# HGRN and mLSTM layer on one core: the second half of the gates' chain one head later, and the low halves of the split weights by VectorE alone

## The chip, the cores and the metric

The kernel runs on 1 core of one Trainium2 chip. The metric is device time in microseconds (us); for one core it is the time of that core. The engines in the text are TensorE (PE, with PEld for its weight loads), VectorE (DVE), ScalarE (ACT), GpSimd (POOL) and SyncE (SP, which issues the DMAs of the weights). All times are us unless marked ns.

## The reference

One layer over 256 latent and 256 context tokens of 1024 channels, all in float32:

```python
sh1, sc1, g1, sh2, sc2, g2 = modulation(c, w_ada, b_ada)       # silu(c) @ w_ada, 6 x 1024
h_lat = rms_norm(x, norm1_g) * (1 + sc1) + sh1                  # the context likewise
p_lat = split(h_lat @ w_in + b_in, SEG_OFFSETS)                 # 13 segments
o_ctx, hs = hgrn_core(p_ctx[0:4], 0)                            # 8 heads, two directions
o_lat     = hgrn_core(p_lat[0:4], hs)                           # S_t = diag(f_t) S_t-1 + k_t v_t
r_ctx, ms = mlstm_core(p_ctx[5:10], 0)                          # 4 heads, conv of width 5 on q and k,
r_lat     = mlstm_core(p_lat[5:10], ms)                         # gates li, lf: cumsum and running max
y = sigmoid(p[11]) * (y_a @ w_branch_a) + sigmoid(p[12]) * (y_b @ w_branch_b)
x = x + g1 * (y @ w_out)
x = x + g2 * hier_moe(rms_norm(x, norm2_g) * (1 + sc2) + sh2)   # 32 experts, top 2 of one group of 8
out = rms_norm(x, final_norm_g)
```

## The kernel before

The program has five stages, which are seen in the trace one behind the other: the prologue (0 to 62 us: norm, first modulation, first weights); the HGRN branch (62 to 300) as four pairs of heads, `hgrn(gp, p, fin)` for p = 0 to 3; the mLSTM branch (300 to 450) as four heads, `mlstm(gp, h, fin)` for h = 0 to 3; the two branch projections, the merge, the output projection and the routing (450 to 575); and the 32 experts (575 to the end), which stream their weights.

**Weights in two halves.** Up to the experts every weight block (128 partitions x 2048 float32, 1 MB, tile `raw`, loaded through SP's queue) is multiplied in three passes: `load_split_` makes a rounded high half `whi` by two ACT copies of 1024 columns (L155), and the low half `wlo = raw - whi` by a subtraction (L158). The subtraction is divided among two engines by `kp`: DVE takes the first 256 * (8 - kp) columns, POOL the rest. `KH`, `MKP` and `GKP` are the `kp` of the HGRN, the mLSTM and the merge blocks. PE then runs `whi` against the high and low halves of the activations (L362 and L363, or L371 and L372 where the tokens are the stationary side) and last `wlo` against the high half (L365, L374). `whi` and `wlo` have two buffers each.

**A pair of HGRN heads** reads five blocks: two for the forget gates (tiles `sg`, `fl`, `fc` on DVE, `kl`, `kc` on POOL), `q`, `v`, and the output gate `s4`. Then `kd` (a scan `scn` on DVE, a product, four transposes on PE at L698 into the PSUM tile "tp") gives the state of the context, and eight levels combine the tokens of the latent sequence: at each, DVE multiplies `xa` (L759) and `kl` (L762), and PE multiplies them (L720, L744, L755). `fin` closes the pair (squares, column sums at L354, `rsn` by DVE L341 and POOL L342, spread by PE L348, then the scaled output) and is issued inside the next pair.

**The modulation pieces.** The rest of w_ada is multiplied on DVE along the way: `ada_dve(b, gp)` loads two blocks and issues eight operations on `adac` (L315 and L317, 128 x 512), and `post`, issued later by `ada_flush`, transposes the sum on PE into "tp" and reduces it on DVE (L326, tile `mod`). "tp" is one PSUM buffer: what PE transposes next into it waits for that reduce. `ADP` says at which place of a pair a chunk stands.

**The gates' chain.** `ml_gates` computes the log gates of all four mLSTM heads as rows of a 40-partition tile (`gz`, in the code `xf`, `li`, `lf`, `fs`): part 1 the logs, part 2 scans, part 3 `r` (`r1`), `R`, `rr`, and `r2`, part 4 the remaining scans, the exponentials on ACT, and the DMA of `rr` to HBM. `ml_cols` transposes the results (through "tp") for the mLSTM heads.

**What sets the order.** A scheduler orders each engine's instructions by priority and by data; `prio(n)` raises or lowers a group, and `tc.issue_after(i)` keeps what stands under it behind instruction i. In the kernel before, parts 1 and 2 of the chain stand behind the gates of p = 2 (`anchor[0]`, `anchor[1]`), and parts 3 and 4 behind the low half of that pair's last block (`anchor[2]`), that is, ahead of its `kd` and its levels.

**An mLSTM head** reads three blocks: q and k (conv, `cz`, on DVE, sigmoid on ACT), v, and the output gate. PE transposes k (L897), ACT makes `wk`, PE multiplies by v, DVE copies the state (`cs`, L908), and PE reads it at L949; the scores (`ex`) follow at L952.

Of the kernel before, what the change touches and what calls it, by code (L numbers as in the profile page):

```python
# [7 lines left out]
F32 = mybir.dt.float32  # L8
# [6 lines left out]
ALU = mybir.AluOpType  # L15
# [4 lines left out]
NQ = NE // 4  # L20
CAP = 32
RZ, RP, RA, RB, RC = 2, 2, 2, 5, 7
KH, MKP, GKP = 2, 3, 2
NWARM, NW0 = 2, (7, 2, 1)
MLG = 2
ADP = (1, 3)
# [115 lines left out]
def view(a, off, pat):  # L142
    return bass.AP(tensor=a.tensor, offset=a.offset + off, ap=[a.ap[0]] + pat)


def body(ctx, tc, A, out, dbg=None):
# [10 lines left out]
    def tt(o, a, b, op, e=None):  # L157
        return (e or V).tensor_tensor(o, a, b, op=op)  # L158

    def prio(n):  # L160
        return tc.high_priority(PRIO[n]) if PRIO[n] else nullcontext()
# [57 lines left out]
    def load_split(src, kp=4, pr="ls_h"):  # L219
        with prio(pr):  # L220
            return load_split_(src, kp)
# [368 lines left out]
    def ml_cols(rs):  # L590
        tps = pmm("tp")
        for a, r_ in enumerate(rs):
            for i in range(2):
                T.transpose(tps[:, 128 * (2 * a + i):128 * (2 * a + i) + 128], r_[:, 128 * i:128 * i + 128], ident)
        act(mlr.rearrange("p a i n -> p (a i n)"), tps, AF.Copy)
# [4 lines left out]
    yah = wp.tile([128, 8, 256], F32R, name="yah", tag="yh")  # L600
    yal = wp.tile([128, 8, 256], F32R, name="yal", tag="yl")

    anchor = []

    def hgrn(gp, p, fin):
        wb = [A["win"][5 * p + j] for j in range(5)]
        bcol = lambda j, m: 10 * p + 2 * j + m
        def ada_at(i):
            for j in range(2):
                if p and ADP[j] == i and 2 + 2 * p + j < 9:  # L610
                    ada_dve(2 + 2 * p + j, gp)

        fl = h1.tile([128, 2, 512], F32, name="fl", bufs=HB)
# [28 lines left out]
                    G.tensor_scalar(kc[:, d, m, :], sn[:, 256:512], oml[:, d, h:h + 1], None, op0=ALU.mult)  # L642
        anchor[:] = [ga.ins, gv.ins]
        ada_at(0)
        w = load_split(wb[2], KH)
        r = pmm("mm")
        q = h1.tile([128, 512], F32, name="q", bufs=1)
# [13 lines left out]
        for i in range(2):  # L661
            r = pmm("mm")
            for j in range(2):
                mm_tok(r[:, 256 * j:256 * j + 256], w, 256 * i + 128 * j)
            tt(v[:, 2 * i:2 * i + 2, :], r.rearrange("p (j n) -> p j n", j=2), br[:, None, :].to_broadcast([128, 2, 256]),
               ALU.add)
        ada_at(1)
        w = load_split(wb[4], KH)
        anchor.append(lolast[0])
        r4 = pmm("mm")  # L670
        s4 = gp.tile([128, 512], F32, name="s4")
        for m in range(2):
# [53 lines left out]
        with prio("lev"):  # L726
            for lv in range(8):
# [28 lines left out]
                    act(acr.rearrange("p a b -> p (a b)"), r, AF.Copy)  # L756
                tb = tot[:, 0, :]
                xv = view(xa[:, 0, :], 0, [[2 * h, 256 // h], [h + 512, 2], [1, h]])
                V.tensor_tensor(xv, xv, view(tb, 1, [[2, 256 // h], [n - 1, 2], [0, h]]), op=ALU.mult)  # L759
                if lv < 7:  # L760
                    yv = view(kl[:, 0, :], 0, [[2 * h, 256 // h], [h + 512, 2], [1, h]])
                    V.tensor_tensor(yv, yv, view(tb, n + 1, [[2, 256 // h], [-n - 1, 2], [0, h]]), op=ALU.mult)  # L762
# [1 line left out]
                    tv = tot.rearrange("p a (n t) -> p a n t", t=2)  # L764
                    tt(t, tv[:, :, :, 0], tv[:, :, :, 1], ALU.mult)
                    tot, n = t, n // 2
        ada_at(3)
        po = pmm("oo")
        for m in range(2):
            o = po[:, 256 * m:256 * m + 256]  # L770
# [28 lines left out]
    with ExitStack() as st:  # L799
        gp = pool(st, "hg")  # L800
        for n, w, b in ([("adac", 512, 1), ("scn", 514, 1), ("kd", 512, 1), ("kt", 512, 1)]
                        + [(f"tot{i}", 512 >> i, 1) for i in range(7)]
                        + [("yk", 512, 2), ("v", 1024, HB), ("s0", 512, 1), ("acr", 512, 1), ("ain", 512, 1), ("adg", 128, 1), ("xa", 1024, 1),
                           ("s4", 512, 1), ("t2", 512, 4)]):
            gp.tile([128, w], F32, name=n, bufs=b)
        zt = gp.tile([128, 256], F32, name="zt")
        G.memset(zt, 0.0)
        lm = gp.tile([128, 5, 32], U8, name="lm")
        lmf = gp.tile([128, 160], F32, name="lmf", tag="v", bufs=HB)
        D.dma_start(lmf, A["lmask"])  # L810
        V.tensor_copy(lm.rearrange("p a b -> p (a b)"), lmf)
        fin = None
        for p in range(4):
            fin = hgrn(gp, p, fin)
            if p == MLG:
                mlrows = []
                gates = ml_gates(mlrows)
                with prio("mlg"), tc.issue_after(anchor[0]), tc.issue_after(anchor[1]):
                    next(gates)
                    next(gates)  # L820
                with prio("mlg"), tc.issue_after(anchor[2]):
                    for _ in gates:
                        pass
                ml_cols(mlrows)
        fin()
        ada_flush()
    h1st.close()
# [14 lines left out]
    def mlstm(gp, h, fin):  # L842
# [13 lines left out]
        q = gp.tile([128, 256], F32, name="q", bufs=2)  # L856
        k = gp.tile([128, 2, 256], F32, name="k", bufs=2)
        with prio("conv"):
            for src, dst, ct in ((qin[:, None, :], q[:, None, :], h), (kin, k, 4 + h)):
                a = dst.shape[1]  # L860
                cw = lambda j: P["cw"][:, 5 * ct + j:5 * ct + j + 1]
                z = gp.tile([128, 2, 256], F32, name="cz")
                z = z[:, 0:a, :]
                V.tensor_scalar(z, src[:, :, 0:256], cw(0), P["cb"][:, ct:ct + 1], op0=ALU.mult, op1=ALU.add)
                for j in range(1, 5):
                    V.scalar_tensor_tensor(z, src[:, :, j:j + 256], cw(j), z, op0=ALU.mult, op1=ALU.add)
                act(dst, z, AF.Sigmoid)
                conv = tt(dst, dst, z, ALU.mult)
        w = load_split(wb[1], MKP, "ls_m")
        br = gp.tile([128, 256], F32, name="br", bufs=2)  # L870
        D.dma_start(br, A["brow"][1024 + 256 * h:1024 + 256 * h + 256].partition_broadcast(128))
# [8 lines left out]
        if fin is not None:  # L880
            fin()
        ada_flush()
        if h % 2 == 0:
            g2acc[0] = gp.tile([128, 512], F32, name="adac")
        with tc.issue_after(conv.ins):
            ada_dve(9 + h // 2, gp, g2acc[0], (h % 2,))
        w = load_split(wb[2], MKP, "ls_m")
        r = pmm("mm")
        s10 = gp.tile([128, 2, 256], F32, name="s10")
# [14 lines left out]
        for d in range(2):  # L904
            rc = pmm("oo")
            for i in range(2):
                T.matmul(rc[:, 0:257], wk[:, d, i, :], v[:, i, :], start=(i == 0), stop=(i == 1))
            V.tensor_copy(cs[:, d, :], rc[:, 0:257])  # L908

        sp = pmm("lv")  # L910
        for i in range(2):
# [573 lines left out]
```

## Time and profile before

| | |
|---|---|
| median of 3 runs | 1005.48 us (1004.79 to 1009.0) |
| profiled execution | 1005.86 us, span 1003.8 us (2.06 us lie around the span) |
| mean granted PE clock | 0.922 |
| busy in the span | PE 862.8, PEld 591.7, DVE 477.0, ACT 277.9, POOL 191.2 us |
| `whi` on ACT | x104, 1052 ns of one |
| `wlo` on DVE, on POOL | x54, 2004 ns of one; x50, 2254 ns of one |

Durations are those of the one profiled execution. A bracket behind an instruction gives how long its engine stood idle before it, and what ended that. A busy PE isn't PE at its peak: where the granted clock is below 1.00, the same matmuls take longer.

### The profile page before, as it was taken

The page shows a single profiled execution, that of the slowest core. Times are in us where ns is not written, and L with a number is a line of the kernel's source. Part 1 is how long each engine was busy: PE and PEld are TensorE (multiplying, and loading weights), DVE is VectorE, ACT ScalarE, POOL GpSimd, SP SyncE. Part 2 cuts the span into 40 slices and gives each one's busy share as a digit, 9 for nine tenths or more (in the row PEclk, how much of TensorE's full clock was granted, in tenths as well). Part 3 has the DMA queues.
Part 4 walks back from the last instruction along what each step waited for, and adds up shares of the span by engine and source line. Part 5 has one row for each costly group of instructions (what it writes and reads, how often), then busy time and mean ns, then how long its engine had stood idle before and what let it go on. Part 6 is the DMA issues. An engine that isn't in the chain of part 4 may idle for free.

```text
span 1003.8 us, 15963 instructions
## 1 busy us (share of the span) xinstructions
PE 862.8 (86%) x6687; PEld 591.7 (59%) x6687; DVE 477.0 (48%) x908; ACT 277.9 (28%) x430; POOL 191.2 (19%) x130
## 2 busy tenths in 40 slices
PE   7999999979998999999999999767686767777865
PEld 3588897968978898999999644213031220313312
DVE  3678779798667988874465422102020110202002
ACT  4564433643323553444443210000000000000101
POOL 0053441535503232124434000000000000000000
PEclk9999999989999999999999999879778776978978
DMA  9733345255243445248887999999999999999996
GB/s 372 287 130 133 126 137 193 98 191 187 96 164 114 165 147 167 83 159 321 300 332 277 373 423 426 426 425 423 428 424 427 425 424 388 419 426 424 426 424 265
DMA packets 45610, 290.50 MB, mean 289 GB/s; under 512 B 5216, under 2 KB 10336, under 8 KB 11104
## 3 DMA queue, kind: packets, MB, share of 16 engines
q1 hardware_dynamic: 45248, 288.94, 72.8%
q8 instruction: 53, 0.87, 0.3%
q10 hardware_dynamic: 288, 0.52, 0.1%
q14 instruction: 21, 0.17, 0.0%
HBM read 288.23 MB, written 1.21 MB: 288 GB/s over the span
## 4 chain that ended last, share of the span: by engine, by line
issue 45%; PE 41%; DVE 8%; ACT 3%; DMA 2%; POOL 1%; SPq 0%; POOLq 0%; DVEq 0%; ACTq 0%
PE mm L365 5%; PE mm L362 5%; PE mm L363 5%; PE mm L374 2%; PE mm L372 2%; PE mm L371 2%; PE mm L1102 2%; PE mm L1099 2%; PE mm L1100 2%; DMA raw<-in_win_dram 2%; PE mm L412 2%; DVE wlo L158 1%; PE mm L1240 1%; ACT whi L155 1%; PE oo L952 1%
## 5 line engine op out<-in xcount | busy, mean ns | idle before, releaser
L158 POOL TENSOR_TENSOR wlo<-raw,whi 128x512 fp32r<-128x512 f32 (+1 forms) x50 | 112.7, 2254 | 197.4 <-ACT whi L155 166.3
L155 ACT ACTIVATE whi<-raw 128x1024 fp32r<-128x1024 f32 x104 | 105.6, 1052 | 104.6 <-POOL wlo L158 26.3
L362 PE MATMUL mm<-hhi,whi 128*128 128x256 f32 (+1 forms) x448 | 132.2, 322 | 0.0
L363 PE MATMUL mm<-hlo,whi 128*128 128x256 f32 (+1 forms) x448 | 130.1, 317 | 0.0
L158 DVE TENSOR_TENSOR wlo<-raw,whi 128x1536 fp32r<-128x1536 f32 (+2 forms) x54 | 108.1, 2004 | 34.1 <-ACT whi L155 30.6
L158 DVE TENSOR_TENSOR a<-a,mm 128x512 f32<-128x512 f32 x8 | 5.5, 688 | 233.5 <-PE mm L1240 233.5
L362 PEld LDWEIGHTS mm<-hhi,whi 128*128 128x128 f32 x448 | 85.5, 191 | 4.8
L363 PEld LDWEIGHTS mm<-hlo,whi 128*128 128x128 f32 x448 | 85.5, 191 | 4.4
L1378 POOL TENSOR_TENSOR rsn<-rsn,con 128x2 f32<-128x2 f32 x1 | 0.7, 698 | 434.7 <-DVE rsn L158 434.7
L365 PE MATMUL mm<-hhi,wlo 128*128 128x256 f32 (+1 forms) x448 | 80.7, 319 | 0.9 <-POOL wlo L158 0.9
L365 PEld LDWEIGHTS mm<-hhi,wlo 128*128 128x128 f32 x448 | 65.8, 191 | 5.8 <-POOL wlo L158 1.1
L1214 DVE SCALAR_TENSOR_TENSOR x<-oo,mod,x 128x256 f32<-128x256 f32 x56 | 24.4, 480 | 88.3 <-PE oo L1273 88.3
L1240 PE MATMUL mm<-ub,xg 128*32 128x512 f32 x304 | 50.3, 734 | 17.3 <-DMA ub<-in_eu_dram 9.9
L371 PE MATMUL mm<-whi,hhi 128*128 128x256 f32 x256 | 63.1, 284 | 0.0
L372 PE MATMUL mm<-whi,hlo 128*128 128x256 f32 x256 | 62.9, 283 | 0.0
L371 PEld LDWEIGHTS mm<-whi,hhi 128*128 128x128 f32 x256 | 49.1, 192 | 0.2
L372 PEld LDWEIGHTS mm<-whi,hlo 128*128 128x128 f32 x256 | 49.1, 192 | 0.1
L155 ACT ACTIVATE aT<-tp 128x512 f32<-128x512 f32 x8 | 4.8, 597 | 148.1 <-PE tp L1252 148.1
L1273 PE MATMUL oo<-owT,y 128*128 128x256 f32 x112 | 35.3, 470 | 8.6 <-ACT y L155 8.6
L1240 PEld LDWEIGHTS mm<-ub,xg 128*32 128x32 f32 x304 | 8.3, 120 | 56.4 <-DMA ub<-in_eu_dram 24.8
L1264 PE MATMUL lv<-uc,aT 128*32 128x512 f32 x280 | 36.1, 604 | 5.6 <-DMA uc<-in_ed_dram 5.6
L1273 PEld LDWEIGHTS oo<-owT,y 128*128 128x128 f32 x112 | 24.6, 230 | 27.4 <-ACT y L155 21.0
(391 smaller groups left out, 1588.3 us busy)
## 6 DMA issues: line engine op xcount, KB each, us to landing
uc<-in_ed_dram SPq DMA_DIRECT2D x35, 1024.0 KB, 19.8
raw<-in_win_dram SPq DMA_DIRECT2D x32, 1024.0 KB, 5.0
raw<-in_wm_dram SPq DMA_DIRECT2D x20, 1024.0 KB, 5.0
ub<-in_eg_dram SPq DMA_DIRECT2D x20, 1024.0 KB, 19.4
ub<-in_eu_dram SPq DMA_DIRECT2D x18, 1024.0 KB, 19.5
raw<-in_wada_dram SPq DMA_DIRECT2D x16, 1024.0 KB, 4.9
uB<-in_eu_dram SPq DMA_DIRECT2D x14, 1024.0 KB, 19.6
uc<-in_eu_dram SPq DMA_DIRECT2D x14, 1024.0 KB, 19.7
```

The lines of the kernel that those rows point to most:

```text
L155: return S.activation(o, i, f, **kw)
L158: return (e or V).tensor_tensor(o, a, b, op=op)
L362: T.matmul(o, a, hhi[:, k, c0:c0 + n], start=(k == 0), stop=False)
L363: T.matmul(o, a, hlo[:, k, c0:c0 + n], start=False, stop=False)
L365: last = T.matmul(o, lo[:, k, 128 * m:128 * m + 128], hhi[:, k, c0:c0 + n], start=False, stop=(k == 7))
L371: T.matmul(o, hhi[:, k, c0:c0 + 128], hi[:, k, :], start=(k == 0), stop=False)
L372: T.matmul(o, hlo[:, k, c0:c0 + 128], hi[:, k, :], start=False, stop=False)
L374: T.matmul(o, hhi[:, k, c0:c0 + 128], lo[:, k, :], start=False, stop=(k == 7))
L1214: V.scalar_tensor_tensor(o, r[:, n * a:n * a + n], mod[:, 0, 40 + c + a:41 + c + a], o, op0=ALU.mult, op1=ALU.add)
L1240: last = T.matmul(r[32 * i:32 * i + 32, :], xg[:, k, 32 * i:32 * i + 32], W[k][:, 512 * i:512 * i + 512], start=(k == 0), stop=(k == 7), t ...
L1264: T.matmul(r[32 * i:32 * i + 32, 0:n], aT[:, k, 32 * i:32 * i + 32], w[k][:, o:o + n], start=(k == 0), stop=(k == 3), tile_position=(0, 32 ...
L1273: last = T.matmul(r[:, 256 * a_:256 * a_ + 256], y[:, 128 * (c + a_):128 * (c + a_) + 128], owT, start=True, stop=True)
```

## The change

`KH` and `MKP` go from 2 and 3 to 0: the low half of every HGRN block after the first two (18 blocks, which had 1536 columns on DVE and 512 on POOL) and of every mLSTM block (12 blocks, 1280 and 768) is one DVE operation of 2048 columns. `GKP` stays at 2. Parts 3 and 4 of the gates' chain, with `ml_cols`, are issued in the pair p = 3 and behind the multiplication of the last level of p = 2 (`level[0]`). The modulation chunk of p = 3 goes from place 1 (ahead of the output gate's block) to place 3, behind that pair's levels. In an mLSTM head the conv of k comes ahead of that of q; the head's half of a modulation chunk moves from behind the conv to behind the copies of `cs`.

```diff
-KH, MKP, GKP = 2, 3, 2
+KH, MKP, GKP = 0, 0, 2
...
-    anchor = []
+    anchor, level, gates, mlrows = [], [None], [None], []
...
-                if p and ADP[j] == i and 2 + 2 * p + j < 9:
+                if p and (ADP[j], 3)[p == 3] == i and 2 + 2 * p + j < 9:
...
         ada_at(0)
+        if p == MLG + 1:
+            with tc.issue_after(level[0]):
+                next(gates[0])
         w = load_split(wb[2], KH)
...
         ada_at(1)
+        if p == MLG + 1:
+            with tc.issue_after(level[0]):
+                next(gates[0], None)
+            ml_cols(mlrows)
         w = load_split(wb[4], KH)
-        anchor.append(lolast[0])
...
-                V.tensor_tensor(xv, xv, view(tb, 1, [[2, 256 // h], [n - 1, 2], [0, h]]), op=ALU.mult)
+                lvl = V.tensor_tensor(xv, xv, view(tb, 1, [[2, 256 // h], [n - 1, 2], [0, h]]), op=ALU.mult)
...
-        ada_at(3)
+        level[0] = lvl.ins
+        with tc.issue_after(level[0]) if p == 3 else nullcontext():
+            ada_at(3)
...
             if p == MLG:
-                mlrows = []
-                gates = ml_gates(mlrows)
+                gates[0] = ml_gates(mlrows)
                 with prio("mlg"), tc.issue_after(anchor[0]), tc.issue_after(anchor[1]):
-                    next(gates)
-                    next(gates)
-                with prio("mlg"), tc.issue_after(anchor[2]):
-                    for _ in gates:
-                        pass
-                ml_cols(mlrows)
+                    next(gates[0])
+                    next(gates[0])
...
-            for src, dst, ct in ((qin[:, None, :], q[:, None, :], h), (kin, k, 4 + h)):
+            for src, dst, ct in ((kin, k, 4 + h), (qin[:, None, :], q[:, None, :], h)):
...
-        if h % 2 == 0:
-            g2acc[0] = gp.tile([128, 512], F32, name="adac")
-        with tc.issue_after(conv.ins):
-            ada_dve(9 + h // 2, gp, g2acc[0], (h % 2,))
         w = load_split(wb[2], MKP, "ls_m")
...
-            V.tensor_copy(cs[:, d, :], rc[:, 0:257])
+            copied = V.tensor_copy(cs[:, d, :], rc[:, 0:257])
+        if h % 2 == 0:
+            g2acc[0] = gp.tile([128, 512], F32, name="adac")
+        with tc.issue_after(copied.ins):
+            ada_dve(9 + h // 2, gp, g2acc[0], (h % 2,))
```

How the instructions stand on VectorE in the pair p = 2, before, from the low half of that pair's last block to the first level (`r`, `rr` and `gz` are the chain, `mod<-tp` is the reduce that frees "tp", the second low half is that of the next pair's first block):

```order
L158 TENSOR_TENSOR wlo<-raw,whi 128x1536
L158 TENSOR_TENSOR r_2442<-gz 8x256 x2
L158 TENSOR_TENSOR gz<-gz 40x256
L570 SCALAR_TENSOR_TENSOR r_2443<-gz 8x128
L568 COPY rr<-gz 8x256 x2
...
L326 TENSOR_REDUCE mod<-tp 128x4
L317 SCALAR_TENSOR_TENSOR adac<-raw,sgc,adac 128x512
L158 TENSOR_TENSOR mod<-mod,pk 128x4
L158 TENSOR_TENSOR wlo<-raw,whi 128x1536
L759 TENSOR_TENSOR xa<-xa,fl 128x256x2
```

And at the same place now:

```order
L158 TENSOR_TENSOR wlo<-raw,whi 128x2048
L158 TENSOR_TENSOR v<-mm,br 128x512
L315 TENSOR_SCALAR adac<-raw,sgc 128x512
L326 TENSOR_REDUCE mod<-tp 128x4
L317 SCALAR_TENSOR_TENSOR adac<-raw,sgc,adac 128x512
L158 TENSOR_TENSOR mod<-mod,pk 128x4
L158 TENSOR_TENSOR wlo<-raw,whi 128x2048
L317 SCALAR_TENSOR_TENSOR adac<-raw,sgc,adac 128x512 x3
L158 TENSOR_TENSOR kd<-kc,scn 128x512
L765 TENSOR_TENSOR xa<-xa,fl 128x256x2
```

The chain is gone from between the two low halves; the reduce stands two operations behind the v addition, and a low half of 2048 columns, three modulation pieces and `kd` stand between it and the first level.

VectorE at the turn from p = 2 to p = 3 now, from the last level's `xa` on (before, neither `r` nor `rr` stood here; `rsn` is the closing step of p = 2):

```order
L765 TENSOR_TENSOR xa<-xa,tot_2374 128x2x2x128
L158 TENSOR_TENSOR wlo<-raw,whi 128x2048
L635 TENSOR_SCALAR fl<-sg,oml,lbt 128x256
L637 TENSOR_SCALAR fc<-sg,oml,lbt 128x256
L158 TENSOR_TENSOR r_2429<-gz 8x256 x2
L158 TENSOR_TENSOR gz<-gz 40x256
L570 SCALAR_TENSOR_TENSOR r_2430<-gz 8x128
L568 COPY rr<-gz 8x256 x2
L570 SCALAR_TENSOR_TENSOR r_2430<-gz 8x128
L573 TENSOR_SCALAR gz<-gz,mle 40x128
L341 TENSOR_SCALAR rsn<-lv 128x4
```

Eight instructions of the chain (two rows are pairs) stand now between the gates of p = 3 and `rsn`.

VectorE in the first mLSTM head before, from the multiplication that ends k's conv to the copies of the state:

```order
L158 TENSOR_TENSOR k<-k,cz 128x512
L315 TENSOR_SCALAR adac<-raw,sgc 128x512
L317 SCALAR_TENSOR_TENSOR adac<-raw,sgc,adac 128x512
L158 TENSOR_TENSOR wlo<-raw,whi 128x1280
L317 SCALAR_TENSOR_TENSOR adac<-raw,sgc,adac 128x512
L908 COPY cs<-oo 128x257
L317 SCALAR_TENSOR_TENSOR adac<-raw,sgc,adac 128x512
L908 COPY cs<-oo 128x257
```

And now, in the same head:

```order
L158 TENSOR_TENSOR k<-k,cz 128x512
...
L158 TENSOR_TENSOR wlo<-raw,whi 128x2048
L869 SCALAR_TENSOR_TENSOR cz<-qin,pk,cz 128x256
L907 COPY cs<-oo 128x257
L869 SCALAR_TENSOR_TENSOR cz<-qin,pk,cz 128x256
L907 COPY cs<-oo 128x257
L315 TENSOR_SCALAR adac<-raw,sgc 128x512
L158 TENSOR_TENSOR q<-q,cz 128x256
```

The modulation pieces stand behind both copies, and pieces of q's conv between them.

## Rows read from the trace of the kernel before

**Rows 1.** Windows by stage; columns: stretch, length, busy time per engine.

```profile
core 0: us, PE busy (x) PEld busy (x) DVE busy (x) ACT busy (x) POOL busy (x), PEclk, DMA share, GB/s
62.00:200.00 138.00, 134.81 (x1331) 119.87 (x1329) 110.02 (x186) 62.32 (x91) 58.17 (x36) 1.00 0.39 133
200.00:222.00 22.00, 15.15 (x162) 13.87 (x160) 21.87 (x33) 11.61 (x17) 9.96 (x5) 0.84 0.46 158
300.00:335.00 35.00, 30.62 (x221) 28.27 (x221) 26.20 (x48) 12.91 (x20) 9.61 (x10) 1.00 0.49 152
575.00:1003.80 428.80, 318.03 (x2076) 110.00 (x2068) 63.67 (x159) 27.99 (x56) 0.70 (x1) 0.83 0.98 413
```

**Rows 2.** Timeline, PE: start, length, instruction, [idle before <- what ended it].

```profile
91.27 0.46 PE L720 MATMUL lv<-xa,yk 128*32 128x32 f32 x32 [0.99 <-DVE xa L759]
...
151.41 0.46 PE L720 MATMUL lv<-xa,yk 128*32 128x32 f32 x32 [1.34 <-DVE xa L759]
...
207.01 0.50 PE L365 MATMUL mm<-hhi,wlo 128*128 128x256 f32 x2 [0.86 <-POOL wlo L158]
...
216.26 1.09 PE L698 MATMUL tp<-con,kd 128*128 128x128 f32 x4 [5.99 <-DVE mod L326]
...
283.02 0.47 PE L720 MATMUL lv<-xa,yk 128*32 128x32 f32 x32 [1.25 <-DVE xa L759]
...
325.92 0.44 PE L897 MATMUL tp<-con,k 128*128 128x128 f32 x2 [2.12 <-DVE k L158]
...
331.15 0.70 PE L949 MATMUL oo<-cs,qi 128*128 128x257 f32 x2 [1.44 <-DVE cs L908]
...
399.60 0.70 PE L949 MATMUL oo<-cs,qi 128*128 128x257 f32 x2 [1.27 <-DVE cs L908]
```

**Rows 3.** Timeline, DVE, pair p = 2: the chain's part and the reduce.

```profile
203.15 4.08 DVE L158 TENSOR_TENSOR r<-gz 8x256 f32<-8x256 f32 x2
207.25 0.42 DVE L158 TENSOR_TENSOR gz<-gz 40x256 f32<-40x256 f32 x1
...
210.03 0.28 DVE L573 TENSOR_SCALAR gz<-gz,mle 40x128 f32<-40x128 f32 x1
...
215.44 0.67 DVE L326 TENSOR_REDUCE mod<-tp 128x4 f32<-128x512 f32 x1
```

**Rows 4.** Timeline, POOL, the same stretch.

```profile
200.95 4.59 POOL L158 TENSOR_TENSOR xa<-fl,q 128x1024 f32<-128x1024 f32 x1 [7.56 <-DVE q L656]
```

**Rows 5.** Windows around that wait, columns as in the first group.

```profile
216.20:219.80 3.60, 3.54 (x74) 3.19 (x75) 3.60 (x5) 3.56 (x5) 1.85 (x1) 0.50 0.91 341
219.80:225.00 5.20, 5.20 (x85) 3.91 (x85) 5.12 (x10) 2.36 (x5) 0.72 (x1) 1.00 1.04 369
```

**Rows 6.** Tile wlo, DVE then POOL, HGRN then mLSTM: ns min/median/max, shapes.

```profile
L158 DVE TENSOR_TENSOR wlo<-raw,whi x19: 1465/1759/3280, 62.6 to 282.7; 128x1536 fp32r<-128x1536 f32 x17, 128x1280 fp32r<-128x1280 f32 x2
L158 POOL TENSOR_TENSOR wlo<-raw,whi x19: 1290/2574/2874, 65.1 to 280.1; 128x512 fp32r<-128x512 f32 x17, 128x768 fp32r<-128x768 f32 x2
...
L158 DVE TENSOR_TENSOR wlo<-raw,whi x13: 1474/1757/3139, 310.5 to 444.2; 128x1280 fp32r<-128x1280 f32 x10, 128x1536 fp32r<-128x1536 f32 x3
L158 POOL TENSOR_TENSOR wlo<-raw,whi x13: 1291/2048/3152, 310.5 to 444.2; 128x768 fp32r<-128x768 f32 x10, 128x512 fp32r<-128x512 f32 x3
```

**Rows 7.** The page, ACT's high halves: last, idle before and what ended most.

```profile
L155 ACT ACTIVATE whi<-raw 128x1024 fp32r<-128x1024 f32 x104 | 105.6, 1052 | 104.6 <-POOL wlo L158 26.3
```

**Rows 8.** Timeline, turn from p = 2 to p = 3, DVE, POOL and PE.

```profile
239.51 2.82 DVE L158 TENSOR_TENSOR wlo<-raw,whi 128x1536 fp32r<-128x1536 f32 x1
242.26 0.56 DVE L635 TENSOR_SCALAR fl<-sg,oml,lbt 128x256 f32<-128x256 f32 x1
...
245.93 0.15 DVE L341 TENSOR_SCALAR rsn<-lv 128x4 f32<-128x4 f32 x1
...
246.17 1.47 POOL L342 TENSOR_TENSOR rsn<-rsn,con 128x4 f32<-128x4 f32 x1 [2.11 <-DVE rsn L341]
...
248.83 1.05 PE L348 MATMUL oo<-con,rsn 128*128 128x128 f32 x8
```

**Rows 9.** Timeline, DVE: the closing step of p = 3, and a modulation piece.

```profile
244.69 0.72 DVE L317 SCALAR_TENSOR_TENSOR adac<-raw,sgc,adac 128x512 f32<-128x512 f32 x1
...
303.85 0.16 DVE L341 TENSOR_SCALAR rsn<-lv 128x4 f32<-128x4 f32 x1 [5.61 <-PE lv L354]
```

More of the change, by code (lines that the diff above doesn't have):

```diff
@@ L867, in mlstm @@
                 act(dst, z, AF.Sigmoid)
-                conv = tt(dst, dst, z, ALU.mult)
+                tt(dst, dst, z, ALU.mult)
         w = load_split(wb[1], MKP, "ls_m")
```

## Prediction

> **What bounds the kernel now.** I read the windows by stage first. From 575 us to the end the DMA share is 0.98 while PE is busy 318.03 of 428.80 us: the experts stream weights at 413 GB/s, and nothing of the change lies there [rows 1]. That stage takes as long as its bytes take, so it can only begin sooner or later: what an earlier stage gains moves the end by as much (buffers limit how much of the stream can be fetched ahead). In the stages that are changed PE is the bound: it works 134.81 of 138.00 us from 62 to 200, but 15.15 of 22.00 from 200 to 222, and 30.62 of 35.00 from 300 to 335 [rows 1]. So I read PE's timeline next, for the idle times and what ended each. Eight waits that the change can touch stand there [rows 2]: 5.99 and 0.86 in the pair p = 2, 0.99, 1.34 and 1.25 before the first level of p = 0, 1 and 3, and 2.12, 1.44 and 1.27 in the mLSTM heads. They make 15.26 us. Third, VectorE's timeline around the longest one shows why: the chain's part 3 holds VectorE from 203.15 to 210.03, two operations of 8x256 alone take 4.08 us there, and the reduce that frees "tp" starts only at 215.44 [rows 3]. PE starts its next transposes at 216.26, when the reduce has ended. Last, the windows around that wait: in the 3.60 us after it PE ran at a granted clock of 0.50, which is its lower level of 1.2 GHz, and only then again at 1.00 [rows 5]. Before it fell the engine had stood idle for those 5.99 us.
>
> **The sum**, against the profiled execution (1005.86 us, which is its span of 1003.8 and 2.06 around it; 0.38 above the median of 1005.48).
>
> A. *The chain leaves the pair p = 2.* Both waits in it go, 5.99 + 0.86 = 6.85, and with the long idle time the stretch at half clock: 3.54 us of PE work at 0.50 take 1.77 at 1.00 [rows 5]. That is 8.62. What is late next is the first level. The pair p = 1, which never had the chain, waits 1.34 us there [rows 2]; to this come a low half that is 0.59 longer (below), and three modulation pieces, which in the new order stand between that low half and `kd`, 3 x 0.72 = 2.16 [rows 9]. New wait 1.34 + 0.59 + 2.16 = 4.09. A = -8.62 + 4.09 = -4.5. Bounds: -8.62 (the pieces fit in time in which VectorE would wait) and -1.9 (a wait long enough to halve the clock once more, 1.77, and another 0.86).
>
> B. *The first levels of p = 0, 1 and 3* wait 0.99 + 1.34 + 1.25 = 3.58 in all. VectorE's low half takes 1759 ns at the median and up to 3280, and POOL's quarter of a block, 1290 at the least, takes 2574 at the median [rows 6]: the two engines hold each other up. Without POOL's share a low half is done when VectorE is done. Nearest rows for its length: 1759 ns (1536 columns, median) and 1465 (1280 columns, the least) make 1.15 ns per column, so 2048 columns take 1759 + 512 x 1.15 = 2350 ns. Before, the block was ready when the slower of the two had ended, 2.57 at the median. B is between -3.58 and +1.8 (three first levels behind a low half that is 0.59 longer). I take -1.5, nearer to the middle since the POOL partner is gone but the DVE operation is longer.
>
> The Trainium skill, page "SBUF — State Buffer", section "Who interferes with whom", says of such pairs that a VectorE instruction with two inputs in SBUF and a GpSimd instruction that reads SBUF shut each other out, and that whoever comes first holds the shared ports to its end. The trace agrees as far as it goes (1290 ns at the least against 2574 at the median on POOL) [rows 6]. By that rule B and C would come out near their lower ends; but by the same rule the longer low halves also hold up POOL's other work (`kl`, `kc`, `xa`), which speaks for the first rival below.
>
> C. *The mLSTM heads*: 2.12 for k's conv, which now comes first, and 1.44 + 1.27 for the copies `cs`, which stood behind a low half and modulation pieces; the pieces now stand behind the copies. In all 4.83. A low half still stands ahead of `cs`, 0.88 longer than before when not held up (2.35 against 1.465). Bounds -4.83 and +1.8 (two copies, each 0.88 later). I take -3.5. Against it: q's conv now comes after k's, and its last product stands behind both copies, so the scores can be late in place of the transposes: 0 to +2.1 (as long as k's wait), I take +0.5.
>
> D. *VectorE's own time.* 18 blocks x 0.59 + 12 x 0.88 = 21.2 us more if none was held up before. The 54 low halves average 2004 ns (the table of the page); by the medians and least values above, with 4 of 1024 columns at 1.17, they would average 1650, so 54 x 0.354 = 19.1 us were spent held up, and 30 of the 50 pairs go: 11.5. Net +9.7. It lies beside PE: in all the time before, PE waited for a low half once, and that was POOL's [rows 2]; and VectorE is busy 110.02 of 138.00 us in the HGRN stage [rows 1]. ACT gains: of its idle time before the high halves, 26.3 us ended with POOL's low half [rows 7] (the buffers of `wlo`). I take 0 on the path; bounds 0 to +9.7.
>
> E. *The turn from p = 2 to p = 3*, where the chain now stands ahead of `rsn`, for which POOL and then PE's L348 wait. Now 6.42 us lie between the start of the low half at 239.51 and `rsn` at 245.93; POOL has it at 246.17 + 1.47 = 247.64, and PE takes it at 248.83, without waiting: 1.19 of slack [rows 8]. After: 2.35 for the low half, 0.56 + 0.53 for the gates, the chain as measured 6.88 (203.15 to 210.03 [rows 3]), from a start that is one piece (0.72) sooner: 9.6, later by 3.2 and by 2.0 beyond the slack. But the 4.08 were measured beside POOL's `xa` of 4.59 us [rows 4], which isn't there at the turn; at 0.42 each, as the `gz` of 40x256 behind them [rows 3], the chain takes 3.64 and nothing is late. Bounds 0 to +2.0, I take +0.7. The modulation chunk of p = 3 now fills VectorE's wait of 5.61 before the last `rsn` [rows 9]: seven pieces stand there, 7 x 0.72 = 5.0, so 0, and were they longer, every us beyond 0.6 would be late at PE. The chain's DMA and `ml_cols` come a pair later but still a whole pair of levels before the first mLSTM head, 0.
>
> Sum: -4.5 - 1.5 - 3.5 + 0.5 + 0 + 0.7 = -8.3, which gives 997.6 us. The likeliest case alone I put at 994 to 1001.
>
> **Rivals.**
> 1. *VectorE becomes the bound* (slower). The longer low halves, which can't be shared out any more, arrive just ahead of the level products and copies for which PE waits, and hold up POOL's `kl` and `kc`, which the levels need too. Then B and C don't come, A is -4.5, and the net +9.7 of D is passed on, with E and q's conv at +0.7 and +0.5: 1012.3. For it: VectorE is busy 21.87 of 22.00 from 200 to 222 [rows 1], and the first levels wait for it already. Against it: without the chain that stretch has some 7 us less, and 0.86 was all that PE ever waited for a low half. It decides from the point at which PE's new waits for VectorE between 62 and 450 us exceed the 17.0 listed (15.26 and the half clock).
> 2. *The stall only moves* (a little faster, or nothing to be measured). A as above, the turn at its upper end (+2.0), B 0, of C only one copy (-1.3), the scores late by 1.5: -2.3, 1003.5. For it: the three places wait for the same engine, and with one instruction early another is late. Against it: at the turn VectorE has no PE behind it for 1.19.
> 3. *Nearly all listed waits go*: 8.62 + 3.58 + 4.83 less p = 1's pattern of 1.34 once = 15.7, 990.2. For it: the two engines no longer stop each other, which shortens more than the rows listed. Against it: the walk in A finds pieces ahead of `kd`.
>
> **How the numbers follow.** Chances: the forecast 0.45, the first rival 0.15, the second 0.22, the third 0.18. Of the median, 0.5% are 5 us, about what a measurement tells from no change. The third rival and most of the forecast lie under 1000.5: faster 0.61. The second, the forecast's upper edge and a mild form of the first lie within: 0.27. Slower 0.12. The range of 8 in 10 runs from 990.5, where the third rival stands, to 1006, which leaves out most of the first.
>
> **What would show it.** In PE's timeline of after: no wait of 5 us at the `kd` transposes of p = 2 and granted clock 1.00 there (A); waits at the first levels under 1 us (B); none over 1 us at the transposes of k and the reads of `cs`, and perhaps one at the scores (C); 2048-column low halves near 2.35 us and rarely longer (D); `rsn` of p = 2 before PE is ready for it, and the idle time of VectorE before the last `rsn` under 1 us (E); the DMA-bound stage beginning some 8 us sooner and as long as before. It is wrong if PE waits for VectorE's low halves at many blocks, if the wait of 6 us comes back at the turn, or if the expert stage begins sooner and ends no sooner.

## The result: 994 us, and the profile after

Four executions of the changed kernel took 991.78 to 995.15 us, 994.06 at the median, against 1006.04 for the kernel before in the same comparison: a ratio of 0.9868 (0.985 to 0.9887). The profiled execution took 991.78 us, 14.1 less than that of before. The forecast was 997.6, the range 990.5 to 1006: the sign and the range hold, the gain was half as large again as forecast (12.0 us between the medians, 8.3 in the sum).

The same windows as in [rows 1], in the profile after:

```profile
62.00:200.00 138.00, 137.46 (x1350) 122.07 (x1348) 111.94 (x192) 66.28 (x95) 37.96 (x27) 1.00 0.39 133
200.00:222.00 22.00, 20.74 (x326) 17.53 (x327) 21.75 (x31) 10.92 (x18) 0.30 (x1) 1.00 0.71 238
...
300.00:335.00 35.00, 35.00 (x243) 32.63 (x242) 30.87 (x62) 15.60 (x25) 1.49 (x4) 1.00 0.59 192
...
575.00:989.60 414.60, 298.99 (x1947) 105.84 (x1945) 61.71 (x154) 26.84 (x55) 0.70 (x1) 0.84 0.98 413
```

PE is busy 137.46, 20.74 and 35.00 us where it was 134.81, 15.15 and 30.62, and the granted clock of the second stretch is 1.00 in place of 0.84. What PE waited for between 62 and 450 us is now this (waits view of the profile after: whom PE waited for, us in all, times, longest):

```profile
PE tp L977 <- DVE rt L973: 2.0, 1, 2.0
PE oo L710 <- ACT kt L155: 1.3, 1, 1.3
PE lv L760 <- DVE kl L768: 0.9, 3, 0.3
PE oo L348 <- POOL rsn L342: 0.9, 1, 0.9
```

All eight waits of [rows 2] are gone; two new ones stand in their place, 1.3 in the pair p = 2 and 2.0 at the output transposes of the last mLSTM head. The last two lines, the waits for `kl` and `rsn`, stood there before too, with 1.1 and 0.8.

To see in which part of the program the time went, I took from PE's timeline of every profile the start of six landmarks (the first `kd` transpose of pairs 0, 1 and 3, the transpose of k of head 1, the first merge matmul, the first expert matmul) and subtracted. The end is the last instruction:

```
                          kd0-kd1  kd1-kd3  kd3-k1   k1-merge  merge-expert  expert-end
before                      61.60   131.70   81.74    124.72       85.14       434.18
changed                     59.95   122.71   76.84    124.85       85.17       434.06
changed, second profile     59.93   122.99   78.42    126.42       85.20       434.35
KH = 0 alone                59.95   125.88   81.54    124.71       85.16       434.21
MKP = 0 alone               61.51   131.99   76.48    123.17       85.15       434.12
KH = MKP = 0 alone          59.97   127.36   77.64    123.16       85.16       434.75
new order alone             61.50   127.42   82.90    126.59       85.16       436.09
POOL fills, old order       60.08   130.35   76.41    123.18       85.17       433.86
changed, chain in p = 2     59.94   126.07   76.80    124.88       85.16       436.26
changed, chunk at place 1   59.95   125.20   75.88    125.98       85.15       434.02
changed, old mLSTM order    59.93   122.84   76.74    123.04       85.17       434.20
changed, modulation back    59.95   122.75   76.48    124.13       85.17       435.06
changed, q's conv first     59.96   122.77   76.57    125.16       85.16       434.03
experiment 6                59.98   122.76   78.37    122.98       83.90       434.94
```

Where the clock is the same, the stretches agree among profiles that share a part to a few tenths, so they tell the parts apart better than whole times do. Some of them hold 3.4 us at a granted clock of 0.50, which costs some 1.6 us (last section): 127.36 and 77.64 with KH = MKP = 0 alone, 82.90 and 126.59 of the new order alone, 78.42 and 126.42 of the second profile, 78.37 of experiment 6; 131.70, 131.99 and 130.35 hold 6.8 us of it. One execution of the kernel with the chunk at place 1 took 1309.3 us at a mean granted clock of 0.557 and is left out of its numbers. From before to after: -1.65, -8.99, -4.90, +0.13, +0.03, -0.12, together -15.5; the first landmark stood 1.3 later in this execution. From the first expert matmul on nothing changes: the start at 555.48 in place of 569.55 moves the end by as much.

```profile
569.55 0.64 PE L1240 MATMUL mm<-uz,xg 128*32 128x512 f32 x4
```

```profile
555.48 0.64 PE L1243 MATMUL mm<-uz,xg 128*32 128x512 f32 x4
```

(the first expert matmul in PE's timeline, before and after.)

### The profile page after: what moved, and what is told of

Read it like the earlier page. It is cut to its first block, busy times and chain, and to the rows that moved or that the text cites. A ratio compares the mean times of both kernels' runs of the same rounds, so it can differ in the third digit from the quotient of the medians.

```text
span 989.6 us, 15886 instructions
## 1 busy us (share of the span) xinstructions
PE 855.5 (86%) x6687; PEld 593.5 (60%) x6687; DVE 463.7 (47%) x908; ACT 277.4 (28%) x430; POOL 122.8 (12%) x100
## 4 chain that ended last, share of the span: by engine, by line
issue 46%; PE 45%; DVE 3%; ACT 3%; DMA 2%; POOL 1%; SPq 0%; POOLq 0%; ACTq 0%; DVEq 0%
PE mm L362 6%; PE mm L363 6%; PE mm L365 6%; PE mm L374 2%; PE mm L372 2%; PE mm L371 2%; PE mm L1105 2%; PE mm L1102 2%; DMA raw<-in_win_dram 2%; PE mm L1103 2%; PE mm L412 2%; PE mm L1243 1%; PE oo L955 1%; PE oo L906 1%; ACT hhi L155 1%
## 5 line engine op out<-in xcount | busy, mean ns | idle before, releaser
L158 DVE TENSOR_TENSOR wlo<-raw,whi 128x2048 fp32r<-128x2048 f32 (+2 forms) x54 | 114.6, 2125 | 38.8 <-ACT whi L155 32.3
L371 PE MATMUL mm<-whi,hhi 128*128 128x256 f32 x256 | 63.2, 284 | 0.0
L158 POOL TENSOR_TENSOR wlo<-raw,whi 128x512 fp32r<-128x512 f32 x20 | 46.4, 2320 | 80.0 <-ACT whi L155 77.1
L371 PEld LDWEIGHTS mm<-whi,hhi 128*128 128x128 f32 x256 | 49.0, 192 | 0.2
L155 ACT ACTIVATE a<-mm 128x512 f32<-128x512 f32 x8 | 4.8, 598 | 127.2 <-PE mm L1243 127.2
```

What stands on the lines that cost most here:

```text
L155: return S.activation(o, i, f, **kw)
L371: T.matmul(o, hhi[:, k, c0:c0 + 128], hi[:, k, :], start=(k == 0), stop=False)
```

## The experiments

Every kernel was timed in five rounds beside the kernel before; "under" and "above" are ratios to it, with their interval.

**1. The parts apart: the new order without the undivided low halves, and the reverse.**

```diff
-KH, MKP, GKP = 0, 0, 2
+KH, MKP, GKP = 2, 3, 2
```

> The changed kernel with KH and MKP back at 2 and 3 (POOL takes a quarter and three eighths of each low half again), all the rest as changed. Theory 1 (the two engines hold each other up, so the undivided low half is ready sooner): the waits of PE before the first levels (3.6 us in all in the kernel before) come back and so do one or two of the mLSTM copies' (1.3 each): 4 to 6 us above the changed kernel, about 999. Theory 2 (the new order alone made the gain, and the longer low halves cost what they save): within 1.5 us of the changed kernel, about 994.

Measured: 1003.74 us, 0.997 (0.9956 to 0.9984). The order alone is worth 0.3%. In the table it gains 4.3 us between kd1 and kd3 and loses 1.2 and 1.9 in the mLSTM heads. These two stretches hold a fall of the clock each; less 1.6 they would be about 81.3 and 125.0, beside 81.74 and 124.72 before, so nothing shows that the order itself gains or loses there. Theory 1 holds (the waits at the first levels are back, 3.8 in all) and its number was too low.

```diff
-KH, MKP, GKP = 2, 3, 2
+KH, MKP, GKP = 0, 0, 2
```

(in the kernel before)

> The kernel before with KH = MKP = 0 alone, order as before. Theory 1: the first levels' 3.6 us and POOL's 0.86 at the last block of p = 2 go, the chain's two operations of 8x256 are a little shorter since POOL does less, the wait at tp stays near 5: 4 to 6 us under the kernel before, about 1001. Theory 2: within 1.5 us of it, about 1006, or slower, since the longer low half stands ahead of the chain in VectorE's order.

Measured: 993.21 us, 0.9865 (0.9848 to 0.9882): one line of numbers gives as much as the whole change. Neither theory had that. The waits view of this kernel:

```profile
PE oo L771 <- DVE xa L759: 2.0, 1, 2.0
PE mm L362 <- DVE v L158: 0.9, 1, 0.9
PE oo L348 <- POOL rsn L342: 0.8, 1, 0.8
PE oo L704 <- ACT kt L155: 0.7, 1, 0.7
...
```

The wait of 5.99 at "tp" isn't among them, though the chain is still in p = 2. Its timeline there, VectorE and one row of POOL, shows the reasons:

```profile
203.01 0.41 DVE L158 TENSOR_TENSOR r<-gz 8x256 f32<-8x256 f32 x1
203.35 0.73 DVE L317 SCALAR_TENSOR_TENSOR adac<-raw,sgc,adac 128x512 f32<-128x512 f32 x1
204.11 0.42 DVE L158 TENSOR_TENSOR r<-gz 8x256 f32<-8x256 f32 x1
```

```profile
197.51 2.46 POOL L158 TENSOR_TENSOR xa<-fl,q 128x1024 f32<-128x1024 f32 x1 [8.86 <-DVE q L656]
```

The two operations that took 4.08 us take 0.41 and 0.42. POOL's `xa`, which lay beside them before and took 4.59 [rows 4], is over here at 199.97, before the low half ahead of the chain begins. And the scheduler, which had other work ready, set modulation pieces between the two.

**2. HGRN or mLSTM: one constant at a time, in the kernel before.**

```diff
-KH, MKP, GKP = 2, 3, 2
+KH, MKP, GKP = 0, 3, 2
```

> The kernel before with KH = 0 alone, MKP still 3. If the HGRN stage carries the gain of the undivided low halves: 9 to 11 us under the kernel before, about 997; the mLSTM waits stay. If the two stages share it evenly: about 1000.

```diff
-KH, MKP, GKP = 2, 3, 2
+KH, MKP, GKP = 2, 0, 2
```

> The kernel before with MKP = 0 alone, KH still 2. If the HGRN stage carries the gain: 3 to 5 us under the kernel before, about 1003, the waits at the transposes of k and the copies going. If evenly: about 1000.

Measured: 999.72 us, 0.9929 (0.9915 to 0.9942), and 1000.46 us, 0.9932 (0.9918 to 0.9945). They share the gain evenly and their sum, 1.39%, is that of both together, 1.35%. In the table KH takes 1.65 and 5.8 from the first two stretches, MKP 5.3 and 1.5 from the next two. The wait at the first level of p = 3 goes with MKP (it is still 1.5 with KH = 0 alone): two blocks of the first mLSTM head are split in the HGRN stage already [rows 6].

**3. Is it POOL's reading? Same order, POOL only writes.**

```diff
...
+                if eng is G and pr != "ls_g":
+                    e = slice(s.stop - 8, s.stop)
+                    tt(lo[:, e], r[:, e], hi[:, e].bitcast(F32), ALU.subtract, eng)
+                    for _ in range(2):
+                        G.memset(lo[:, s].bitcast(F32), 0.0)
+                    continue
```

> The kernel before, its order kept, but POOL's share of the HGRN and mLSTM low halves is not subtracted: POOL reads only 8 columns of each half and then fills its 512 or 768 columns twice with zeros (about 1.1 us, as long as the subtraction alone), so that part of the low halves is left out. VectorE's instructions and their order are the same. Theory 1 (POOL's reads and VectorE's two-input operations shut each other out): VectorE's low halves fall to 1.76 and 1.47 us, the two chain operations of 8x256 to 0.4 each, the waits at the first levels nearly go, the wait at tp in p = 2 falls by about 4 of 6: 992 to 996 us. Theory 2 (the place of the chain in VectorE's order is what costs): the wait at tp stays over 4 us and the time over 1002.

Measured: 997.26 us, 0.9901 (0.9886 to 0.9916), between the theories. The table says where each is right. In the stretches kd0-kd1, kd3-k1 and k1-merge this kernel stands at 60.08, 76.41 and 123.18, as the kernels with undivided halves do, though VectorE's order is that of before and POOL is nearly as busy (181.0 us): the waits at the first levels and in the mLSTM heads came from POOL's reads. Between kd1 and kd3 it gains 1.35 of KH's 5.8 only. By estimate 1.5 us of what is missing are the clock: of 6.8 us at 0.50 in that stretch PE works 6.50, where it worked 3.54 before [rows 5]. Waits, then timeline of VectorE and of POOL in that pair:

```profile
PE tp L704 <- DVE mod L332: 2.8, 1, 2.8
PE mm L371 <- POOL gz L582: 2.6, 1, 2.6
```

```profile
202.43 3.09 DVE L158 TENSOR_TENSOR r<-gz 8x256 f32<-8x256 f32 x2
```

```profile
200.23 4.59 POOL L158 TENSOR_TENSOR xa<-fl,q 128x1024 f32<-128x1024 f32 x1 [9.57 <-DVE q L662]
204.72 0.44 POOL L158 TENSOR_TENSOR wlo<-raw,whi 128x8 fp32r<-128x8 f32 x1
205.22 1.11 POOL L237 MEMSET wlo<- 128x512 f32 x2
206.26 0.09 POOL L582 MEMSET gz<- 40x1 f32 x1
```

The chain's two operations still take 3.09, since POOL's `xa` of 4.59 us still lies beside them; and POOL's part of the low half stands in POOL's queue behind `xa`, whoever reads what. (The wait of 2.6 is for that part, which L371 multiplies; it is put down to the `gz` of 0.09 us that follows on POOL.) So there the old order has its share: the stall at "tp" is a long POOL read, the chain behind it on VectorE, and the reduce behind the chain.

**4. The chain back in p = 2, in the changed kernel.**

```diff
-        if p == MLG + 1:
-            with tc.issue_after(level[0]):
-                next(gates[0])
...
-        if p == MLG + 1:
-            with tc.issue_after(level[0]):
-                next(gates[0], None)
-            ml_cols(mlrows)
...
+        anchor.append(lolast[0])
...
+                with prio("mlg"), tc.issue_after(anchor[2]):
+                    for _ in gates[0]:
+                        pass
+                ml_cols(mlrows)
```

> The changed kernel with parts 3 and 4 of the gates' chain back in p = 2 behind its last low half, all the rest as changed. Theory 1 (the reduce that frees tp stands behind the chain in VectorE's order): the wait at the kd transposes of p = 2 comes back with 4 to 6 us and the granted clock falls to 0.50 behind it: 6 to 8 us above the changed kernel, about 1001. Rival (without POOL beside it the chain is short enough, its 8x256 operations near 0.4 us each instead of 2.0): wait under 2 us, clock stays at 1.00, 1 to 3 us above, about 996.

Measured: 995.62 us, 0.9894 (0.9869 to 0.9918), beside 0.9868 and 0.9859 for the changed kernel: 1.6 and 1.9 us above by the medians, 2.6 and 3.5 by the ratios, about what the rival had, though the intervals overlap. No wait at "tp" comes back; PE's longest in that pair is 2.0, behind the levels. The stretch kd1-kd3 is 126.07 in place of 122.71, so the move is worth 3.4 us there (4.3 with POOL's share, experiment 1); the clock stays at 1.00.

**5. The mLSTM heads' order, in the changed kernel:** both back, the modulation half alone, the conv alone; with them the changed kernel again, and the chunk of p = 3 back at place 1.

```diff
-            for src, dst, ct in ((kin, k, 4 + h), (qin[:, None, :], q[:, None, :], h)):
+            for src, dst, ct in ((qin[:, None, :], q[:, None, :], h), (kin, k, 4 + h)):
...
-                tt(dst, dst, z, ALU.mult)
+                conv = tt(dst, dst, z, ALU.mult)
...
-        with tc.issue_after(copied.ins):
+        with tc.issue_after(conv.ins):
             ada_dve(9 + h // 2, gp, g2acc[0], (h % 2,))
```

(with the last three lines, and what opens the tile, moved ahead of the load of `wb[2]`)

> The changed kernel with the mLSTM heads' order as before: q's conv first, the modulation half ahead of the copies. Theory 1: waits at the transposes of k (2.1) and before the copies (1.4, 1.3) come back, the new wait of 2.0 at the last head's output transposes may go: 2 to 5 us above the changed kernel, about 997. Rival (those waits came from POOL's share of the low halves and went with it): within 1 us, about 994.

> The changed kernel with the modulation half of an mLSTM head back behind the conv, k's conv still first. Theory 1 (the pieces behind the copies stand between the scores of the last head and its denominators on VectorE): the wait of 2.0 before the last head's output transposes goes, 2 to 4.5 us under the changed kernel, about 990. Theory 2 (k's conv first is what costs): within 1 us of the changed kernel, 994.

> The changed kernel with q's conv first again, the modulation half behind the copies as changed. Theory 1: within 1 us of the changed kernel, 994, with the wait of 2.0 still there. Theory 2: 2 to 4.5 us under it, about 990.

> The changed kernel itself once more, as the baseline of this group of runs. All theories: 994 us at the median, PE's wait of about 2 us before the output transposes of the last mLSTM head there again.

```diff
-                if p and (ADP[j], 3)[p == 3] == i and 2 + 2 * p + j < 9:
+                if p and ADP[j] == i and 2 + 2 * p + j < 9:
...
-        with tc.issue_after(level[0]) if p == 3 else nullcontext():
-            ada_at(3)
+        ada_at(3)
```

> The changed kernel with the modulation chunk of p = 3 back at place 1, ahead of its last block. Theory 1 (the place matters little since VectorE has slack there either way): within 1 us of the changed kernel, 994. Rival (its eight pieces come back ahead of the levels of p = 3 and beside the chain): 2 to 4 us above, 997, with a wait at the kd transposes or the first level of p = 3.

Measured: both back 989.52 us, 0.9829 (0.9815 to 0.9844); the modulation half back 991.14, 0.9837 (0.982 to 0.9854); the conv back 991.52, 0.985 (0.9829 to 0.9872); the changed kernel again 993.68, 0.9859 (0.9838 to 0.9879); chunk at place 1 993.42, 0.9867 (0.9846 to 0.9888). So the mLSTM part of the change costs 4.2 to 4.5 us by the medians and 3.0 to 3.9 by the ratios. The interval of both back is clear of the first interval of the changed kernel and overlaps the second at its edge, but all five executions with both back (988.92 to 989.95) lie under all nine of the changed kernel (991.19 to 995.15). One part back alone isn't clear of the changed kernel. The profiles show 1.8 us of it, between k1 and the merge (124.85 against 123.04); that the rest is the clock, which can fall behind the new wait (last section), is argued and not shown. The piece that the profile explains is the modulation half. VectorE in the last head, profile after:

```profile
417.55 0.43 DVE L907 COPY cs<-oo 128x257 f32<-128x257 f32 x1
417.89 0.74 DVE L317 SCALAR_TENSOR_TENSOR adac<-raw,sgc,adac 128x512 f32<-128x512 f32 x1
418.55 0.15 DVE L958 TENSOR_SCALAR dn<-oo 128x1 f32<-128x1 f32 x1
...
418.95 0.74 DVE L317 SCALAR_TENSOR_TENSOR adac<-raw,sgc,adac 128x512 f32<-128x512 f32 x1
...
421.35 0.16 DVE L961 RECIPROCAL dn<-dn 128x1 f32<-128x1 f32 x1
```

and with both back:

```profile
418.04 0.43 DVE L911 COPY cs<-oo 128x257 f32<-128x257 f32 x1
...
418.90 0.16 DVE L958 TENSOR_SCALAR dn<-oo 128x1 f32<-128x1 f32 x1
...
419.54 0.17 DVE L961 RECIPROCAL dn<-dn 128x1 f32<-128x1 f32 x1
```

Four pieces, two of them shown, stand between the last copy and the reciprocal of the denominators (`dn`), which starts 3.8 us behind that copy instead of 1.5, and PE waits the 2.0 seen above. With the modulation half back that wait is 0.2. What the conv's order alone costs isn't shown: the profile with q first has the same waits as the changed one, and its stretch up to the merge is no shorter (125.16); with the modulation half back, q first is worth 1.1 there (124.13 and 123.04). The chunk's place is worth 2.5 us between kd1 and kd3, of which 1.0 comes back before k1, and nothing that the medians tell.

**6. The best parts together:** undivided halves, chain and chunk as changed, the mLSTM order of before, and the merge blocks undivided too.

```diff
-KH, MKP, GKP = 0, 0, 2
+KH, MKP, GKP = 0, 0, 0
```

(in the kernel with both back)

> The changed kernel with the mLSTM order of the kernel before (989.5 so far) and GKP = 0 as well, so that the 20 merge blocks are subtracted by VectorE alone. Theory 1: the merge stage keeps PE busy 122 of 125 us already, so at most 1 to 2 us are to be had: 988. Rival (VectorE's 2.3 us low halves are late there): 990 to 992.

Measured: 989.25 us, 0.9815 (0.9801 to 0.9828). It beats both kernels; GKP itself adds 1.3 us in the stretch merge-expert (83.90 against 85.17), as theory 1 had it, and its interval overlaps that of the kernel with both back.

## Why the prediction was right, and where its reasons were not

**What bounds.** Right: the gain was PE's waits before 450 us and the half clock behind one of them, and the expert stage passed it on one to one. In the sum's own terms the trace after gives A -8.62 + 1.26 = -7.36, B -3.58, C -4.83 + 1.96 = -2.87, and 0 for D and E, together -13.8, where the profiled execution gained 14.1. The forecast's -8.3 held A and B too small, both on the same side, and the median of 994.06 lies at the very edge of its own 994 to 1001. The range held because it was drawn out to the third rival.

**A, the chain out of p = 2 (-4.5).** The place was right, the new wait was not. It was put at 4.09, at `xa`; it is 1.26, at the product behind the `kd` transposes. Its copy `kt` stands on ACT behind two copies of `whi`, which had waited for a modulation piece. ACT, then PE, then VectorE after:

```profile
208.04 2.01 ACT L155 ACTIVATE whi<-raw 128x1024 fp32r<-128x1024 f32 x2 [5.44 <-DVE adac L317]
209.95 0.58 ACT L155 ACTIVATE kt<-tp 128x512 f32<-128x512 f32 x1
```

```profile
210.58 0.60 PE L710 MATMUL oo<-v,kt 128*128 128x128 f32 x3 [1.26 <-ACT kt L155]
```

```profile
200.50 2.25 DVE L158 TENSOR_TENSOR wlo<-raw,whi 128x2048 fp32r<-128x2048 f32 x1
...
203.29 0.47 DVE L315 TENSOR_SCALAR adac<-raw,sgc 128x512 f32<-128x512 f32 x1
203.68 0.67 DVE L326 TENSOR_REDUCE mod<-tp 128x4 f32<-128x512 f32 x1
...
205.01 2.27 DVE L158 TENSOR_TENSOR wlo<-raw,whi 128x2048 fp32r<-128x2048 f32 x1
```

The reduce starts at 203.68, where it started at 215.44 [rows 3]; the pieces that were counted on the path fit in. That the move alone gains 4.3 in that stretch, with POOL's share kept, is near the forecast's 4.5 by luck: the sum left out that the chain was long (4.08 for two small operations [rows 3]) because POOL was reading beside it [rows 4], which it counted only at the turn, in E.

**B, the first levels (-1.5).** Mis-sized: all 3.58 went. The bounds held, the value taken was too near the middle. The sum asked when the block is ready, but PE waited for `xa`, and what held `xa` up differs by pair: for p = 0 the low half ahead of it, 2.79 us; for p = 1 a modulation piece ahead of it, 1.77; for p = 3 `xa` itself, 2.58.

```profile
87.62 2.79 DVE L158 TENSOR_TENSOR wlo<-raw,whi 128x1536 fp32r<-128x1536 f32 x1
...
148.49 1.77 DVE L317 SCALAR_TENSOR_TENSOR adac<-raw,sgc,adac 128x512 f32<-128x512 f32 x1
...
280.29 2.58 DVE L759 TENSOR_TENSOR xa<-xa,fl 128x512 f32<-128x512 f32 x1 [0.59 <-PE lv L720]
```

In the profile after, the first and the last of them (the piece of p = 1 stands elsewhere):

```profile
88.92 2.27 DVE L158 TENSOR_TENSOR wlo<-raw,whi 128x2048 fp32r<-128x2048 f32 x1
...
270.62 1.13 DVE L765 TENSOR_TENSOR xa<-xa,fl 128x512 f32<-128x512 f32 x1 [0.23 <-PE lv L726]
```

With 512 columns more, the low half of p = 0 is done sooner. Over all blocks one of 2048 columns takes 2290 ns at the median, where 2350 were estimated:

```profile
L158 DVE TENSOR_TENSOR wlo<-raw,whi x20: 2255/2290/3402, 64.3 to 299.9; 128x2048 fp32r<-128x2048 f32 x20
```

**C, the mLSTM heads (-3.5 + 0.5).** The size is near (-2.9) by luck, the mechanism was wrong. The waits of 4.83 went with MKP alone, in the old order; the new order brings nothing (experiment 1) and puts one wait of 2.0 in the last head. That wait was looked for at the scores of q, and stands behind the modulation pieces that were moved.

**D, VectorE's own time (0 on the path, +9.7 busy).** The 0 on the path held; the count behind it is the step that failed. VectorE's busy time didn't rise by 9.7, it fell by 13.3. Its low halves did rise, from 108.1 to 114.6 us, so all the rest fell by 19.8. The profile page's busy line after:

```profile
PE 855.5 (86%) x6687; PEld 593.5 (60%) x6687; DVE 463.7 (47%) x908; ACT 277.4 (28%) x430; POOL 122.8 (12%) x100
```

The sum counted by how much POOL held up the low halves, not everything else that VectorE did beside POOL: the 49 modulation pieces took up to 1941 ns and take 898 at most, the chain's `r` and `rr` 5.66 together and now 1.52. In the kernel with the new order and POOL's share one sees it plainly: a piece that takes 0.47 above takes 2.07, an addition on 128x4 takes 1.25 in place of 0.14, beside POOL's `xa` and its part of a low half.

```profile
203.51 2.07 DVE L315 TENSOR_SCALAR adac<-raw,sgc 128x512 f32<-128x512 f32 x1
...
207.18 1.25 DVE L158 TENSOR_TENSOR mod<-mod,pk 128x4 f32<-128x4 f32 x1
```

ACT's wait for POOL [rows 7] went too; its largest now is for PE:

```profile
L155 ACT ACTIVATE whi<-raw 128x1024 fp32r<-128x1024 f32 x104 | 105.8, 1053 | 125.6 <-PE mm L363 27.5
```

**E, the turn (+0.7).** The lower bound, 0. DVE, POOL and PE after, to be read beside [rows 8]:

```profile
229.80 2.28 DVE L158 TENSOR_TENSOR wlo<-raw,whi 128x2048 fp32r<-128x2048 f32 x1
...
232.94 0.94 DVE L158 TENSOR_TENSOR r<-gz 8x256 f32<-8x256 f32 x2
...
235.88 0.15 DVE L341 TENSOR_SCALAR rsn<-lv 128x4 f32<-128x4 f32 x1
```

```profile
236.12 1.60 POOL L342 TENSOR_TENSOR rsn<-rsn,con 128x4 f32<-128x4 f32 x1 [1.66 <-DVE rsn L341]
```

```profile
239.51 1.05 PE L348 MATMUL oo<-con,rsn 128*128 128x128 f32 x8
```

From the low half to `rsn` 6.08 us, 6.42 before, with the chain between them: alone it takes 2.94. The chunk in the last wait of p = 3 left 0.49 of VectorE's 5.61 [rows 9], as forecast.

```profile
293.43 0.16 DVE L341 TENSOR_SCALAR rsn<-lv 128x4 f32<-128x4 f32 x1 [0.49 <-PE lv L354]
```

**The rivals.** The first (VectorE the bound) is refuted by the kernel with KH = MKP = 0 alone. The second (the stall only moves, 1003.5) is out: no execution of the changed kernel took over 995.15. The third had the mechanism: nearly all listed waits went, and more operations got shorter than the rows listed. Its figure, 990.2, is reached by the parts together (989.25) and not by this change, which has the new wait of 2.0. The Trainium skill, page "SBUF — State Buffer", section "Who interferes with whom", says that a VectorE instruction with two SBUF inputs contends with a GpSimd instruction that reads SBUF and not with one that only writes it. Experiment 3 agrees: beside POOL's zeros the low half of p = 0 takes 1.74 us where it took 2.79, the modulation pieces 954 ns at most where they took 1941, and the stretches are 60.08, 76.41 and 123.18 us where they were 61.60, 81.74 and 124.72. The tensor_scalar of 2.07 us above has one SBUF tensor input and was held up too; the section allows that in the modes in which it takes both ports, and no run here shows the mode.

## What to carry to other kernels

The share of VectorE's work that was given to POOL here was paid for by operations of VectorE that had no part in the split (`xa`, the modulation pieces, the chain). So ask of such a split what POOL's reads do to the small operations in VectorE's queue, and try it undivided first: here one line of constants was worth as much as the whole change. Price the parts of a change apart even when they have one aim; here one part (the mLSTM order) cost 3 to 4.5 us that the others covered. Landmarks subtracted within one profile tell parts apart to some tenths, where the whole times of one kernel spread over 1.0 to 7.6 us; look first whether the clock fell in the stretch.

## What had not been expected of the hardware

The clock falls behind the same short waits in one execution and not in another. The profile after has a granted clock of 1.00 all through the changed stages; in the second profile of the same kernel it fell behind the waits of 0.88 and 1.95 us at `rsn` and at the last head's transposes. Its windows of these two stretches, columns as in [rows 1]:

```profile
294.30:297.70 3.40, 3.40 (x18) 3.40 (x18) 1.32 (x3) 0.00 (x0) 0.57 (x4) 0.50 0.71 280
...
430.80:434.20 3.40, 3.40 (x18) 3.40 (x18) 2.71 (x4) 1.16 (x3) 0.00 (x0) 0.51 0.25 53
```

Each cost about 1.6 us in the table (78.42 against 76.84, 126.42 against 124.85): nearly twice the wait of 0.88 once more, and less than the wait of 1.95. In the profiles of all kernels the wait at `rsn`, 0.79 to 0.88 us, was followed by such a fall in four of 14, that at the last head's transposes, 1.88 to 1.96, in two of six. Two falls would be most of the spread of this kernel, 991.19 to 995.15, and the three kernels with the modulation half back, which lack the wait of 1.95, varied by 1.0, 1.8 and 2.0 us. That the clock explains the other executions, which have no profile, is argued and not shown.
